# A Winograd convolution: the fourth input pair by SyncE's queue in fp32, the fifth's casting load issued later

## The chip, the cores and the metric

The kernel runs on one core of a Trainium2 chip. The metric is the device time of one execution in microseconds (us), the median of three runs. A profile of one execution, taken by the hardware profiler, goes with it.

## The reference

A 3x3 convolution with padding 1, stride 1, no bias: 16 images of 64 channels, 64 x 64 pixels, to 128 channels. Inputs and output are fp32.

```python
batch, c_in, h, w, c_out = 16, 64, 64, 64, 128
x_pad = np.pad(x, ((0, 0), (0, 0), (1, 1), (1, 1)), mode='constant')
...
output[b, co] += weight[co, ci, kh, kw] * x_pad[b, ci, kh:kh+h, kw:kw+w]
```

The input is 16.8 MB, the output 33.6 MB.

## The kernel before

**Pairs.** Two images of 64 channels fill the 128 partitions, so there are 8 pairs, counted from index 0 in the code ("the fourth pair" is index 3). One pair is 2.10 MB of fp32, 16 KB in each partition. Each image of a pair is multiplied with 64 rows of TensorE.

**The transform.** The convolution is taken two output rows at a time. The input rows stay in fp16 in `xs[p]`; `ss[p]` holds the sums of the row pairs (rows 2j and 2j+1). The weights are combined once into five groups in `Wt` (G0, G21, G1, G01, G2). For each pair there are four blocks (`blk`) of 8 row pairs. A block computes three products for both images: U (G1 on `ss`), A (G21 and G0 on `xs`) and Bt (G01 and G2 on `xs`), each in a PSUM tile `acc` for each image; one line, L174, holds all these matmuls. ScalarE copies U to `ut` (L188); VectorE adds A + U into the even output rows (L196) and Bt + U into the odd ones (L199) of the output tile `ot`.

**The input's two ways.** The first three pairs come in fp32 by SyncE's queue into tiles `x0`, `x1`, `x2` of the pool `opool` (L43 to L47), and are cast to `xs` on the chip, in pieces of 16 rows (L104): pair 0 by ScalarE and GpSimd, pairs 1 and 2 by ScalarE alone, at blocks that the table `later` names. The other five pairs come by loads that GpSimd issues and that cast to fp16 on the way (`load`, L60): indices 3 and 4 after GpSimd's own casts of pair 0, indices 5 to 7 behind the sums of the third pair. `load(q, H)` is one transfer of a whole pair, `load(q, H // 2)` two of half a pair.

**Sums.** Pair 0's sums are made on VectorE. GpSimd makes those of pair p + 1 at the start of the loop's turn p, in two halves (L73), from the fp32 tile where there is one in `raws`, else from `xs`.

**Output.** `opool` has seven buffers of 16 KB in a partition, shared by the fp32 input tiles and the output tiles `ots` (two for each pair, one for each image). They are handed out in turn, so that an output tile waits for whatever used its buffer seven tiles earlier. Image 0 of a pair is stored by SyncE's queue, image 1 by ScalarE's, the latter one block late (`held`). Most stores are a whole image (2.10 MB); image 0 of the first pair and both images of the last are stored in halves (`cuts_of`).

**Order.** The framework places the waits between engines; `keep(...)` holds an instruction in program order on its engine. `spool` has three buffers for `ss`, `xpool` eight for `xs`, so no `xs` is reused.

Of the kernel before, what the change touches and what calls it, by code (L numbers as in the profile page):

```python
# [8 lines left out]
F32 = mybir.dt.float32  # L9
F16 = mybir.dt.float16  # L10
# [3 lines left out]
def kernel(  # L14
# [6 lines left out]
    nc = tc.nc  # L21
    B, CI, H, W = x.shape
    CO = weight.shape[0]
    assert H == 64 and W == 64 and CI == 64 and CO == 128 and B % 2 == 0
    NP = B // 2
# [3 lines left out]
    x_rows = x.rearrange("b c h w -> (b c) h w")  # L29
# [5 lines left out]
    xpool = ctx.enter_context(tc.tile_pool(name="xpool", bufs=8))  # L35
    opool = ctx.enter_context(tc.tile_pool(name="opool", bufs=7))
# [7 lines left out]
    x1 = opool.tile([128, H, W], F32, tag="ot", name="x1")  # L44
    nc.sync.dma_start(x1, x_rows[128:256, :, :])
    x2 = opool.tile([128, H, W], F32, tag="ot", name="x2")
    nc.sync.dma_start(x2, x_rows[256:384, :, :])  # L47
    raws = {1: x1, 2: x2}
    ident = const.tile([128, 128], F16)
    make_identity(nc, ident)  # L50
    w16 = const.tile([CO, CI * 9], F16)
    keep(nc.gpsimd.tensor_copy(w16, w_raw))  # L52

    xs = {p: xpool.tile([128, H, W], F16, tag="xs", name="xs") for p in range(3)}

    def load(p, rows):
        xs[p] = xpool.tile([128, H, W], F16, tag="xs", name="xs")
        for lo in range(0, H, rows):
            keep(
                nc.gpsimd.dma_start(  # L60
                    xs[p][:, lo : lo + rows, :],
                    x_rows[128 * p : 128 * p + 128, lo : lo + rows, :],
                )
            )
# [3 lines left out]
    def sums(eng, p, src, lo, n):  # L68
        if p not in ss:
            ss[p] = spool.tile([128, H // 2, W], F16, tag="ss", name="ss")  # L70
        v = src.rearrange("p (j i) c -> p j i c", i=2)
        keep(
            eng.tensor_add(  # L73
                ss[p][:, lo : lo + n, :], v[:, lo : lo + n, 0, :], v[:, lo : lo + n, 1, :]
            )
        )
# [26 lines left out]
    def cast(copy, p, src, lo, hi):  # L103
        keep(copy(xs[p][:, lo:hi, :], src[:, lo:hi, :]))  # L104
# [5 lines left out]
    keep(nc.scalar.copy(wrow(G2), wps[2]))  # L110
    cast(nc.gpsimd.tensor_copy, 0, x0, 34, 50)
    cast(nc.gpsimd.tensor_copy, 0, x0, 50, 64)
    for p in (3, 4):
        load(p, H)
    later = {
        (0, 0): [(0, x0, 18, 34)],
        (0, 2): [(1, x1, 0, 16), (1, x1, 16, 32)],
        (0, 3): [(1, x1, 32, 48), (1, x1, 48, 64)],
    }
    later.update({(1, n): [(2, x2, 16 * n, 16 * n + 16)] for n in range(4)})  # L120

    held = []

# [4 lines left out]
    def store(eng, p, b2, ot, lo, hi):  # L128
        return eng.dma_start(
            out_rows[2 * p + b2, :, lo:hi, :],  # L130
            ot.rearrange("p j i c -> p (j i) c")[:, lo:hi, :],
        )

    for p in range(NP):
        if p + 1 < NP:
            for lo in (0, 16):
                sums(nc.gpsimd, p + 1, raws.get(p + 1, xs[p + 1]), lo, 16)
                if (p, lo) == (1, 16):
                    for q in range(5, NP):
                        load(q, H if q == 5 else H // 2)  # L140
        ots = [
            opool.tile([128, H // 2, 2, W], F32, tag="ot", name="ot") for _ in range(2)
        ]
        for blk in range(4):
            j0 = blk * RB

            def group(wi_rows):

                tiles = [
                    psum.tile([128, RB, W], F32, tag="acc", name="acc") for _ in range(2)  # L150
                ]
                n = 3 * len(wi_rows)
                i = 0
                for wi, off in wi_rows:
                    for kw in (1, 0, 2):
                        c_lo, c_hi = max(0, 1 - kw), min(W, W + 1 - kw)
                        for b2 in range(2):
                            p0 = 64 * b2
                            lo, hi = j0, j0 + RB
                            if off is None:  # L160
                                rhs = ss[p][p0 : p0 + 64, lo:hi, c_lo + kw - 1 : c_hi + kw - 1]
                            else:
                                while 2 * lo + off < 0:
                                    lo += 1
                                while 2 * (hi - 1) + off > H - 1:
                                    hi -= 1
                                first = 2 * lo + off
                                last = 2 * (hi - 1) + off
                                rhs = xs[p][
                                    p0 : p0 + 64,  # L170
                                    first : last + 1 : 2,
                                    c_lo + kw - 1 : c_hi + kw - 1,
                                ]
                            nc.tensor.matmul(  # L174
                                tiles[b2][:, lo - j0 : hi - j0, c_lo:c_hi],
                                Wt[p0 : p0 + 64, wi, kw, :],
                                rhs,
                                start=i == 0,
                                stop=i == n - 1,
                            )  # L180
                        i += 1
                return tiles

            U = group([(G1, None)])
            us = []
            for b2 in range(2):
                ut = upool.tile([128, RB, W], F32, tag="ut", name="ut")
                keep(nc.scalar.copy(ut, U[b2]))  # L188
                us.append(ut)
            while held and (p, blk) != (1, 0):  # L190
                keep(store(nc.scalar, *held.pop(0)))
            for piece in later.get((p, blk), ()):
                cast(nc.scalar.copy, *piece)
            A = group([(G21, 1), (G0, -1)])
            for b2 in range(2):
                nc.vector.tensor_add(ots[b2][:, j0 : j0 + RB, 0, :], A[b2], us[b2])  # L196
            Bt = group([(G01, 0), (G2, 2)])
            for b2 in range(2):
                nc.vector.tensor_add(ots[b2][:, j0 : j0 + RB, 1, :], Bt[b2], us[b2])  # L199
            if blk in cuts_of[p][0]:  # L200
                store(nc.sync, p, 0, ots[0], *cuts_of[p][0][blk])
            if blk in cuts_of[p][1]:
                held.append((p, 1, ots[1], *cuts_of[p][1][blk]))
# [32 lines left out]
```

## Time and profile before

| what | value |
|---|---|
| median of 3 runs | 125.97 us (125.95 to 126.64) |
| the profiled execution's own time | 126.62 us |
| its span, first to last instruction | 124.8 us |
| TensorE busy | 108.0 us (86% of the span) |
| VectorE, ScalarE, GpSimd busy | 84.5, 46.5, 38.6 us |
| HBM read, written | 17.07 MB, 33.55 MB |
| transfers, share of 16 engines: SyncE's, ScalarE's, GpSimd's queue | 45.0%, 31.7%, 20.8% |
| mean granted TensorE clock | 0.961 |

The queues appear in the profile as q1 (SyncE), q10 (ScalarE) and q0 (GpSimd). Their MB are bytes written: a casting load of a pair counts 1.05 MB although it reads 2.10 MB. The share of 16 engines is the time that a queue's packets took, as a part of what the core's 16 transfer engines had. The profiled execution lies 0.65 us above the median; 1.8 us of its time lie outside its span. Windows are given in us from the start of the span.

### The profile page before, as it was taken

What the parts mean: (1) busy time and instruction counts of PE and PEld (TensorE: products, weight loads), DVE (VectorE), ACT (ScalarE), POOL (GpSimd) and SP (SyncE); (2) the same over time, 40 slices, a digit from 0 to 9 for tenths busy, and PEclk for the clock granted to TensorE, in tenths of its full rate; (3) what the DMA queues carried; (4) which work ended last, traced back from release to release, by engine and by line L of the source; (5) the groups of instructions that cost most, each with busy time, mean ns of one, the idle gap of its engine ahead of it and who ended that gap; (6) DMA issues with size and microseconds to landing.
All of it is one profiled execution on the core that took longest, in us unless ns stands there. A gap on an engine that the chain in (4) does not pass through costs nothing.

```text
span 124.8 us, 2430 instructions
## 1 busy us (share of the span) xinstructions
PE 108.0 (86%) x984; PEld 49.8 (40%) x984; DVE 84.5 (68%) x135; ACT 46.5 (37%) x78; POOL 38.6 (31%) x30
## 2 busy tenths in 40 slices
PE   0699999999999999999999999999999999990000
PEld 0544444444444444444444444444444444430000
DVE  1019987877777887888777778777877787774000
ACT  4118559966653333333333333333333333330000
POOL 2219780799975001910240032004200510000000
PEclk9999999999999999999999999999999999999555
DMA  5899999999999999999999999999999999999991
GB/s 163 367 430 451 430 302 247 278 276 312 365 344 333 341 370 385 382 392 375 370 381 386 382 400 369 354 406 400 374 369 404 425 420 430 420 420 430 428 404 68
DMA packets 4330, 45.52 MB, mean 365 GB/s; under 512 B 480, under 2 KB 480, under 8 KB 1120
## 3 DMA queue, kind: packets, MB, share of 16 engines
q1 hardware_dynamic: 2016, 23.36, 45.0%
q10 hardware_dynamic: 1296, 16.78, 31.7%
q0 software_dynamic: 1008, 5.24, 20.8%
q8 instruction: 7, 0.11, 0.3%
q14 instruction: 3, 0.02, 0.0%
HBM read 17.07 MB, written 33.55 MB: 406 GB/s over the span
## 4 chain that ended last, share of the span: by engine, by line
PE 86%; DMA 2%; DVE 1%; issue 1%; POOL 1%; DVEq 0%
PE acc L174 81%; PE warm L97 3%; DMA w_raw<-in_weight_dram 2%; PE wp L91 1%; DVE ot L196 1%; POOL w L52 1%; DVEq L231 0%; DVE ot L199 0%; DVEq L196 0%
## 5 line engine op out<-in xcount | busy, mean ns | idle before, releaser
L174 PE MATMUL acc<-xs,Wt 64*128 64x504 f16 (+3 forms) x768 | 87.0, 374 | 0.0
L174 PEld LDWEIGHTS <-Wt 64*128 64x128 f16 x960 | 46.9, 95 | 56.2 <-issue 0.9
L188 ACT COPY ut<-acc 128x512 f32<-128x512 f32 x64 | 34.4, 589 | 56.9 <-issue 39.0
L196 DVE TENSOR_TENSOR ot<-acc,ut 128x512 f32<-128x512 f32 x64 | 41.2, 685 | 20.8 <-PE acc L174 18.4
L199 DVE TENSOR_TENSOR ot<-acc,ut 128x512 f32<-128x512 f32 x64 | 41.1, 683 | 0.0
L73 POOL TENSOR_TENSOR ss<-xs 128x1024 f16<-128x1024 f16 x10 | 21.1, 2130 | 49.3 <-DMA xs<-in_x_dram 49.3
L174 PE MATMUL acc<-ss,Wt 64*128 64x504 f16 (+1 forms) x192 | 26.0, 377 | 0.0
L104 ACT CAST xs<-x 128x1024 f16<-128x1024 f32 (+1 forms) x10 | 10.5, 1070 | 3.3 <-DMA x<-in_x_dram 3.3
L73 POOL TENSOR_TENSOR ss<-x 128x1024 f16<-128x1024 f32 x4 | 9.4, 2358 | 5.0 <-DMA x<-in_x_dram 5.0
L73 DVE TENSOR_TENSOR ss<-x 128x512 f16<-128x512 f32 x4 | 3.3, 868 | 7.5 <-DMA x<-in_x_dram 7.5
L91 PE MATMUL wp<-ident,w 128*64 128x128 f16 x18 | 1.3, 328 | 4.3 <-POOL w L52 4.3
L104 POOL CAST xs<-x 128x1024 f16<-128x1024 f32 (+1 forms) x2 | 3.0, 1518 | 4.5 <-DMA x<-in_x_dram 4.5
L97 PE MATMUL warm<-blank 128*128 128x400 f32 x6 | 4.2, 864 | 0.0
L60 POOL DMA_DIRECT2D xs<-in_x_dram x7 | 3.9, 574 | 0.0
L91 PEld LDWEIGHTS <-w 128*64 128x64 f16 x18 | 1.1, 210 | 4.3 <-POOL w L52 4.3
L97 PEld LDWEIGHTS warm<-blank 128*128 128x128 f32 x6 | 1.8, 326 | 1.4 <-issue 1.3
L98 ACT CAST Wt<-wp 128x384 f16<-128x384 f32 x1 | 0.5, 478 | 3.0 <-PE wp L91 3.0
L98 ACT ACT_TABLE_LOAD x1 | 1.3, 1283 | 0.7 <-PEq L220 0.7
L52 POOL CAST w<-w_raw 128x576 f16<-128x576 f32 x1 | 0.7, 663 | 2.3 <-DMA w_raw<-in_weight_dram 2.3
L94 DVE MEMSET blank<- 128x400 f32 x1 | 0.4, 392 | 0.9 <-PEq L220 0.9
L109 ACT CAST Wt<-wp 128x384 f16<-128x384 f32 x1 | 0.5, 478 | 0.5 <-DVE Wt L101 0.5
L100 DVE TENSOR_TENSOR Wt<-wp,Wt 128x384 f16<-128x384 f32 x1 | 0.6, 551 | 0.0
(8 smaller groups left out, 1.9 us busy)
## 6 DMA issues: line engine op xcount, KB each, us to landing
out_dram<-ot ACTq DMA_DIRECT2D x7, 2048.0 KB, 19.0
out_dram<-ot SPq DMA_DIRECT2D x6, 2048.0 KB, 18.3
x<-in_x_dram SPq DMA_DIRECT2D x3, 2048.0 KB, 12.0
out_dram<-ot SPq DMA_DIRECT2D x4, 1024.0 KB, 12.6
xs<-in_x_dram POOLq DMA_DIRECT2D x3, 1024.0 KB, 22.0
xs<-in_x_dram POOLq DMA_DIRECT2D x4, 512.0 KB, 51.2
out_dram<-ot ACTq DMA_DIRECT2D x2, 1024.0 KB, 11.1
w_raw<-in_weight_dram SPq DMA_DIRECT2D x1, 288.0 KB, 2.8
```

What stands on the lines that cost most here:

```text
L52: keep(nc.gpsimd.tensor_copy(w16, w_raw))
L60: nc.gpsimd.dma_start(xs[p][:, lo : lo + rows, :], x_rows[128 * p : 128 * p + 128, lo : lo + rows, :],)
L73: eng.tensor_add(ss[p][:, lo : lo + n, :], v[:, lo : lo + n, 0, :], v[:, lo : lo + n, 1, :])
L91: nc.tensor.matmul(wp[q : q + 64, k * CO : k * CO + CO], w16[:, t::9], ident)
L97: nc.tensor.matmul(warm[:, 0:400], blank[:, 0:128], blank)
L98: keep(nc.scalar.copy(wrow(G1), wps[1]))
L100: keep(nc.vector.tensor_sub(wrow(G21), wps[2], wrow(G1)))
L104: keep(copy(xs[p][:, lo:hi, :], src[:, lo:hi, :]))
L174: nc.tensor.matmul(tiles[b2][:, lo - j0 : hi - j0, c_lo:c_hi], Wt[p0 : p0 + 64, wi, kw, :], rhs, start=i == 0, stop=i == n - 1,)
L188: keep(nc.scalar.copy(ut, U[b2]))
L196: nc.vector.tensor_add(ots[b2][:, j0 : j0 + RB, 0, :], A[b2], us[b2])
L199: nc.vector.tensor_add(ots[b2][:, j0 : j0 + RB, 1, :], Bt[b2], us[b2])
```

## The change

The fourth pair (index 3) is loaded in fp32 into a further `opool` tile `x3` by SyncE's queue, right behind `x2`; its cast to `xs[3]` is done by ScalarE in four pieces in the four blocks of pair index 2, and GpSimd makes its sums from `x3`. The fifth pair's casting load (index 4) is issued behind the second pair's sums (loop turn 0) instead of ahead of the loop. The loads of indices 5 to 7 stay behind the third pair's sums and keep their sizes. The output tiles move by one place in the turn of the seven buffers.

```diff
     x2 = opool.tile([128, H, W], F32, tag="ot", name="x2")
     nc.sync.dma_start(x2, x_rows[256:384, :, :])
-    raws = {1: x1, 2: x2}
+    x3 = opool.tile([128, H, W], F32, tag="ot", name="x3")
+    nc.sync.dma_start(x3, x_rows[384:512, :, :])
+    raws = {1: x1, 2: x2, 3: x3}
...
-    xs = {p: xpool.tile([128, H, W], F16, tag="xs", name="xs") for p in range(3)}
+    xs = {p: xpool.tile([128, H, W], F16, tag="xs", name="xs") for p in range(4)}
...
-    for p in (3, 4):
-        load(p, H)
...
-    later.update({(1, n): [(2, x2, 16 * n, 16 * n + 16)] for n in range(4)})
+    for p in (2, 3):
+        later.update({(p - 1, n): [(p, raws[p], 16 * n, 16 * n + 16)] for n in range(4)})
...
                 sums(nc.gpsimd, p + 1, raws.get(p + 1, xs[p + 1]), lo, 16)
-                if (p, lo) == (1, 16):
-                    for q in range(5, NP):
-                        load(q, H if q == 5 else H // 2)
+                if lo == 16 and p < 2:
+                    for q in ((4,), range(5, NP))[p]:
+                        load(q, H if q < 6 else H // 2)
```

## The prediction

> **What bounds the kernel now.** I read the chain of waits first, because it names the engine that seems to set the end:
>
> ```profile
> PE 86%; DMA 2%; DVE 1%; issue 1%; POOL 1%; DVEq 0%
> ```
>
> Taken alone this says TensorE. But TensorE's last instruction lies near 113 us and the span is 124.8 us, so I read the slices and the queue table of the page next:
>
> ```profile
> PE   0699999999999999999999999999999999990000
> DMA  5899999999999999999999999999999999999991
> ...
> q1 hardware_dynamic: 2016, 23.36, 45.0%
> q10 hardware_dynamic: 1296, 16.78, 31.7%
> q0 software_dynamic: 1008, 5.24, 20.8%
> ```
>
> TensorE is busy without a gap and then stops; the transfer engines go on for about 10 us more. The three queues' packets take 45.0 + 31.7 + 20.8 = 97.5% of 16 engines' span. q1 is SyncE's queue (fp32 loads, half of the stores), q10 ScalarE's (the other stores), q0 GpSimd's (casting loads). The table of windows shows how full the transfer engines are stage by stage (the last two columns are their share and the GB/s written):
>
> ```profile
> 5.00:15.00 10.00, 10.00 (x68) 4.67 (x66) 6.22 (x10) 5.46 (x9) 5.44 (x5) 1.00 1.02 436
> 15.00:30.00 15.00, 15.00 (x144) 6.89 (x142) 12.37 (x21) 10.18 (x15) 10.77 (x10) 1.00 1.01 282
> 30.00:50.00 20.00, 20.00 (x192) 9.21 (x190) 15.37 (x25) 9.12 (x16) 8.98 (x5) 1.00 1.02 356
> 50.00:100.00 50.00, 50.00 (x472) 22.92 (x470) 39.26 (x63) 16.17 (x31) 11.76 (x6) 1.00 1.02 386
> 100.00:113.00 13.00, 12.30 (x116) 5.47 (x112) 10.24 (x18) 4.29 (x8) 0.34 (x1) 1.00 1.00 425
> 113.00:121.00 8.00, 0.00 (x0) 0.00 (x0) 0.67 (x2) 0.00 (x0) 0.00 (x0) 0.64 1.01 426
> ```
>
> From 5 to 121 us the share is never under 1.00. The end is the end of the transfers. How much TensorE could slip before it matters comes from the transfers after 113 us:
>
> ```profile
> DMA packets 544, 3.86 MB, mean 322 GB/s; under 512 B 74, under 2 KB 74, under 8 KB 74
> ...
> out_dram<-ot SPq DMA_DIRECT2D x1, 1024.0 KB, 10.5
> out_dram<-ot ACTq DMA_DIRECT2D x1, 1024.0 KB, 10.2
> ```
>
> The last two stores, 1.05 MB each, are issued at 113.1 and 113.7 us. 3.86 - 2.10 = 1.76 MB were still queued ahead of them, 1.76 MB / 426 GB/s = **4.1 us of backlog**. A compute delay below that costs nothing at the end; a change in transfer work counts in full.
>
> **The change, part by part.**
>
> *The fourth pair's transfer.* Both forms read 2.10 MB of fp32 from HBM; the casting form writes 1.05 MB, the SyncE form 2.10 MB. From the windows of the transfers: in 15 to 30 us q0 took 62.6% of 15 us for 1.85 MB, 5.08 us per MB written, so the fourth pair's casting load cost 1.049 x 5.08 = 5.33 us of all 16 engines. (Over 30 to 100 us it is 23.6% of 70 us for 3.39 MB, 4.87 us per MB, 5.11 us a pair.) An fp32 load on q1 in 5 to 15 us: 101.9% of 10 us for 4.36 MB, 2.34 us per MB, 2.10 x 2.34 = 4.90 us. In 15 to 30 us q1, shared with casts, paid 38.3% of 15 us for 2.36 MB, 2.43 us per MB, 5.10 us a pair. The saving lies between 5.11 - 5.10 = 0.0 and 5.33 - 4.90 = 0.43 us. Most of the new load runs while SyncE's queue is alone, as in the 5 to 15 us row, and what it replaces ran in the 15 to 30 us row, so I take 0.4 us. Upper bound with everything around it: source bytes moved in 15 to 30 us are 4.23 + 1.85 = 6.08 MB, 405 GB/s against 436 before it; if the whole stretch ran at 436, it would save 15 x (1 - 405/436) = 1.07 us.
>
> *The fifth pair's issue* moves from 12.3 us (L60 after the two POOL casts at L104) to behind the second pair's sums. Rows:
>
> ```profile
> 13.73 4.68 POOL L73 TENSOR_TENSOR ss<-x 128x1024 f16<-128x1024 f32 x2 [0.75 <-DMA x<-in_x_dram]
> 22.63 4.68 POOL L73 TENSOR_TENSOR ss<-x 128x1024 f16<-128x1024 f32 x2 [4.23 <-DMA x<-in_x_dram]
> 27.26 2.69 POOL L60 DMA_DIRECT2D xs<-in_x_dram  x5
> ```
>
> The two POOL issues at 11.74 us took 1.24 us; without them the second pair's sums (data landed 13.7) still wait for their data, so nothing is gained there. The fifth's load is issued at about 18.4 us and takes 0.56 us of POOL. The third pair's fp32 no longer shares the engines: the first two landed at 8.8 and 13.7 us, so it lands near 18.7 instead of 22.6. Its sums run to about 23.9, and the loads of pairs 6 to 8 go out about 3.5 us earlier. No cost: the sums for the fourth pair need ss[0]'s slot and x3, the fifth's the cast load; both land long before TensorE needs them (50 and 63 us).
>
> *Casts.* Four ScalarE pieces of 1.06 us (L104) join blocks (2,0) to (2,3), 4.2 us. The same pieces sit in blocks (1,0) to (1,3) now, and TensorE runs on there without a gap; ScalarE then idles 1.2 us a block. The sums of pair 4 read fp32: 2 x (2.36 - 2.12) = 0.5 us more of POOL, which waits 49.3 us for loads in all. If that cover were gone, the casts would still have the 4.1 us of backlog. SyncE's extra issue is 0.43 us at 2.5 us, ahead of nothing but the store at 17.15 us.
>
> *The stores behind x3.* This is the real risk. In 50 to 75 us the queues take turns packet by packet: nearly equal counts, half the time for the half-size loads:
>
> ```profile
> q1 hardware_dynamic: 289, 4.21, 40.2%
> q10 hardware_dynamic: 291, 4.24, 39.9%
> q0 software_dynamic: 299, 1.09, 21.6%
> ```
>
> So a queue progresses by rounds. Eight packets per engine make a pair's transfer: 4.90 / 8 = 0.61 us a whole fp32 packet, half that for half-tile stores, 5.2 / 8 = 0.65 us a casting one. Now the first image's half stores (issued 17.15 and 23.9 us) land 13.0 and 18.9 us later, at 30.2 and 42.8. With x3 ahead of them: x3 runs alone from 18.7 until casting packets appear, 3.3 us after the issue as now (issued 11.74, first packets after 15), at 21.7; the remaining 1.9 us then goes at half rate, to 25.4. First half store: two rounds of 0.31 + 0.65 to 27.4, where ScalarE's store joins, then six of 0.31 + 0.61 + 0.65 = 1.57, to 36.8; second: eight more of 1.57, or of 1.24 once half-size casts follow (0.31 + 0.61 + 0.33), so it ends at 48.5 to 49.4 and lands, some 0.8 us later, at **49.3 to 50.2 us**. The same count for the kernel before gives 42.4 against the 42.8 shown. Its `ot` slot is taken again by the second image of pair index 3, whose first addition starts at 50.22 + 0.61 = 50.8 us:
>
> ```profile
> 50.22 1.29 DVE L196 TENSOR_TENSOR ot<-acc,ut 128x512 f32<-128x512 f32 x2 [0.58 <-ACT ut L188]
> ```
>
> The margin shrinks from 8.0 us to 0.6 to 1.5 us. Next comes SyncE's store of pair index 1, eight rounds of 0.61 + 0.61 + 0.33: near 62 us, needed at 50.8 + 12.8 = 63.6. I cost it at nothing; a miss of 2 us would be hidden by the backlog.
>
> *Sum:* -0.4 us of transfer work, +0 elsewhere. The profiled execution took 126.62 us (124.8 of span, 1.8 around it), giving 126.2; it is 0.65 above the median of 125.97. Against the median: **125.6 us**. I take 1% (1.26 us) as what a measurement of this kernel can tell from no change.
>
> **The rivals.**
>
> *A. The mixed stretch clears up: faster.* The 405 GB/s in 15 to 30 us may be what whole-pair casting loads, one behind the other, cost everything beside them. Then the full 1.07 us comes back, and with it the slower part of 30 to 50 us, where the sixth pair's whole-pair load runs (356 GB/s written and 1.38 MB of casts, 425 GB/s of source bytes; 20 x (1 - 425/436) = 0.5 us): 125.97 - 1.6 = 124.4. For it: no other stretch is as slow, and in it both q0 and q1 cost more per MB than elsewhere. Against: the fifth and sixth pairs' whole-pair casts still run from 21.7 us on.
>
> *B. A late slot: slower.* Place: vector addition L196 of pair index 3, second image, waiting for the second half store. If x3's eight packets share three ways (0.61 + 0.65 + 0.61 = 1.87 us each), the store is late by 15 us instead of 7: 57.8 us. DVE then waits 7.0 us, PSUM tiles aren't freed, TensorE stops, and every later store shifts. It counts beyond 4.1 us: 125.97 + 2.9 - 0.4 = 128.5; a store landing at 56.5 gives 127.2. Against: ScalarE's first store is issued only at 26.7 us, after x3 is nearly in.
>
> *C. Written bytes count: slower.* If the engines' price follows the bytes written, x3 costs 1.05 MB more at 436 GB/s, 2.4 us: 128.4. Against: 15 to 30 us writes only 282 GB/s at a share of 1.01, so casts fill the engines by what they read. The Trainium skill, "DMA: Bandwidth & Descriptors", section "Where 436 GB/s comes from", says the SBUF ports bind at 435 GB/s; by that rule this rival would hold wherever the ports are full. The trace agrees with the ceiling (436 in 5 to 15 us) but shows the engines full far below it under casts.
>
> *D. Nothing at all:* the packets cost the same either way, 126.0. This lies inside the forecast's own range.
>
> **How the numbers follow.** Forecast with D, 125.6, own range 125.0 to 126.6: 0.56. A: 0.19. B: 0.15, spread from 126.8 to 128.5. C: 0.10. Faster by over 1% needs A: 0.19. Slower by over 1% (over 127.2) needs C or most of B: 0.23; within 1%: 0.58. The range reaches to A's end and into half of B: 124.3 to 127.7.
>
> **What would show it.** Right: the transfer share stays at 1.00 from 5 to 121 us; q0 falls by 1.05 MB and about 4.3% of the span, q1 rises by 2.10 MB and 4%; the third pair's sums start near 18.7 instead of 22.6; the second half store takes about 26 us to land; TensorE still ends near 113. Wrong: L196 or TensorE with more than 4 us of idle time released by out_dram (B); q1's cost per MB above 2.5 us while x3 moves (C); 15 to 30 us at 425 GB/s of source bytes or more (A).

## The result and the profile after

The changed kernel takes **136.4 us** (median of 6 runs, 136.18 to 137.99) against 126.17 us for the kernel before in the same runs: 1.083 times as long, 95% interval 1.077 to 1.089. The prediction was 125.6 us. Its profiled execution took 136.34 us, 134.6 us of it span.

The chain of waits of the changed kernel, shares by engine and by line (PE is TensorE, DVE VectorE, ACT ScalarE, POOL GpSimd; L175, L197 and L200 are L174, L196 and L199 of the kernel before):

```profile
PE 67%; DMA 20%; DVE 3%; issue 1%; DVEq 1%; POOL 1%
PE acc L175 63%; DMA out_dram<-ot 18%; PE warm L99 3%; DMA w_raw<-in_weight_dram 2%; DVE ot L197 2%; PE wp L93 1%; DVE ot L200 1%; POOL w L54 1%; DVEq L232 0%; DVEq L197 0%
```

An output store now has 18% of the chain, and it was not in it before. In order of time (start, length, what; "..." where pieces are left out) the chain shows which store:

```profile
10.20 11.82 PE acc L175 x108
...
23.99 24.34 DMA out_dram<-ot
...
48.86 0.70 DVE ot L197
...
49.60 72.99 PE acc L175 x638
```

The store issued at 23.99 us is the second half of pair index 0's first image, on SyncE's queue. It lands 24.34 us later, at 48.33 us, and releases an addition into an output tile, which releases TensorE. VectorE's timeline names the place (start, length, and in brackets the idle time before it and what ended it):

```profile
38.06 0.69 DVE L197 TENSOR_TENSOR ot<-acc,ut 128x512 f32<-128x512 f32 x1 [0.70 <-POOL ss L75]
48.86 0.69 DVE L197 TENSOR_TENSOR ot<-acc,ut 128x512 f32<-128x512 f32 x1 [10.10 <-DMA out_dram<-ot]
```

These are the first two additions of block (2,0): the first image's at 38.06 us, the second image's after a wait of 10.1 us. In the kernel before the two stand together:

```profile
37.46 1.29 DVE L196 TENSOR_TENSOR ot<-acc,ut 128x512 f32<-128x512 f32 x2 [0.63 <-PE acc L174]
```

The table of waits of the changed kernel adds what followed on TensorE (total, times, longest):

```profile
DVE ot L197 <- DMA out_dram<-ot: 10.1, 1, 10.1
PE acc L175 <- DVE ot L197: 8.3, 1, 8.3
```

The stages, as the table of windows shows them for the changed kernel (length, busy time of PE, of its weight loads, of DVE, ACT and POOL, then granted TensorE clock, share of the transfer engines, GB/s written):

```profile
30.00:50.00 20.00, 11.71 (x110) 5.05 (x106) 7.75 (x13) 8.15 (x12) 5.70 (x3) 0.86 1.02 355
50.00:100.00 50.00, 50.00 (x450) 25.05 (x448) 38.27 (x62) 17.99 (x32) 12.61 (x6) 0.95 0.88 333
100.00:113.00 13.00, 13.00 (x126) 6.62 (x122) 10.05 (x17) 4.29 (x8) 0.00 (x0) 1.00 0.77 324
```

Up to 50 us the transfer engines are as full as before while TensorE stands still. Then the stores that were not computed in time are missing, and the casting loads take their place: from 50 to 75 us GpSimd's queue writes 1.78 MB, where it wrote 1.09 MB before (packets, MB, share).

```profile
q0 software_dynamic: 499, 1.78, 35.5%
```

From 75 to 100 us it has nothing left to write, where it wrote 0.91 MB before, and between the late stores the engines run dry: 0.12 x 50 + 0.23 x 13 = 9.0 us idle from 50 to 113 us, of the 9.8 us by which the span grew (134.6 - 124.8).

TensorE's granted clock also fell, some 3 us into the stop that began at 41.3 us. In windows of 1 us it was 1.00 from 43 to 44 us, 0.73 from 44 to 45, 0.50 from 45 to 54, 0.65 from 54 to 55, and 1.00 from 55 us on. So the matmuls that started again at 49.60 us ran at half the clock for about 5 us:

```profile
45.00:50.00 5.00, 0.40 (x3) 0.14 (x4) 1.14 (x2) 0.00 (x0) 0.00 (x0) 0.50 1.03 392
50.00:55.00 5.00, 5.00 (x28) 2.12 (x26) 3.23 (x6) 1.72 (x3) 0.00 (x0) 0.53 1.01 385
```

The last addition of the whole kernel ends 11.5 us later than before, at 125.2 instead of 113.7 us:

```profile
112.39 1.28 DVE L199 TENSOR_TENSOR ot<-acc,ut 128x512 f32<-128x512 f32 x2
123.89 1.28 DVE L200 TENSOR_TENSOR ot<-acc,ut 128x512 f32<-128x512 f32 x2
```

TensorE's stop is 8.3 us of this. Half of the 5 us at half the clock, 2.5 us, is an estimate for the slow restart, and the loop's first matmul started 0.5 us later than in the chain of the kernel before (10.20 against 9.74 us); together that is 11.3 us.

So the open question was: why does a tile of pair index 2 wait for a store of pair index 0, when the prediction had that store's buffer used again only by pair index 3, 12.8 us later?

### The profile page after: what moved, and what is told of

It reads as the page before. It is cut to its first block, busy times and chain, and to the rows that moved or that the text cites. A ratio compares the mean times of both kernels' runs of the same rounds, so it can differ in the third digit from the quotient of the medians.

```text
span 134.6 us, 2434 instructions
## 1 busy us (share of the span) xinstructions
PE 111.1 (83%) x984; PEld 54.0 (40%) x984; DVE 84.6 (63%) x135; ACT 50.4 (37%) x82; POOL 38.5 (29%) x29
## 4 chain that ended last, share of the span: by engine, by line
PE 67%; DMA 20%; DVE 3%; issue 1%; DVEq 1%; POOL 1%
PE acc L175 63%; DMA out_dram<-ot 18%; PE warm L99 3%; DMA w_raw<-in_weight_dram 2%; DVE ot L197 2%; PE wp L93 1%; DVE ot L200 1%; POOL w L54 1%; DVEq L232 0%; DVEq L197 0%
## 5 line engine op out<-in xcount | busy, mean ns | idle before, releaser
L175 PE MATMUL acc<-xs,Wt 64*128 64x504 f16 (+3 forms) x768 | 93.8, 379 | 8.3 <-DVE ot L197 8.3
L175 PEld LDWEIGHTS <-Wt 64*128 64x128 f16 x960 | 51.0, 96 | 63.6 <-issue 12.0
L197 DVE TENSOR_TENSOR ot<-acc,ut 128x512 f32<-128x512 f32 x64 | 41.3, 685 | 32.1 <-PE acc L175 18.9
L200 DVE TENSOR_TENSOR ot<-acc,ut 128x512 f32<-128x512 f32 x64 | 41.1, 683 | 0.0
L175 PE MATMUL acc<-ss,Wt 64*128 64x504 f16 (+1 forms) x192 | 31.3, 386 | 0.0
L75 POOL TENSOR_TENSOR ss<-xs 128x1024 f16<-128x1024 f16 x8 | 16.8, 2122 | 39.1 <-PE acc L175 19.6
L106 ACT CAST xs<-x 128x1024 f16<-128x1024 f32 (+1 forms) x14 | 14.7, 1066 | 3.1 <-DMA x<-in_x_dram 3.1
L75 POOL TENSOR_TENSOR ss<-x 128x1024 f16<-128x1024 f32 x6 | 14.1, 2365 | 2.4 <-DMA x<-in_x_dram 2.4
L62 POOL DMA_DIRECT2D xs<-in_x_dram x6 | 3.4, 579 | 0.0
```

The costliest lines, as they stand in the source:

```text
L62: nc.gpsimd.dma_start(xs[p][:, lo : lo + rows, :], x_rows[128 * p : 128 * p + 128, lo : lo + rows, :],)
L75: eng.tensor_add(ss[p][:, lo : lo + n, :], v[:, lo : lo + n, 0, :], v[:, lo : lo + n, 1, :])
L175: nc.tensor.matmul(tiles[b2][:, lo - j0 : hi - j0, c_lo:c_hi], Wt[p0 : p0 + 64, wi, kw, :], rhs, start=i == 0, stop=i == n - 1,)
```

## The experiments

**The program's own waits** gave the theory. In the instruction list of the changed kernel, the late addition waits on the completion of two transfers, the sixth and seventh issued on the SyncE and ScalarE queues (counting w as number 1 and x3 as number 5): the two half stores of pair index 0's first image. Listing all first writes to output tiles with the transfers that they wait for gives who took whose buffer (s00 is the store of pair index 0's image 0, and so on):

```
            before             changed
pair 2      x0, x1             x1, s00
pair 3      s00, s01           s01, x2
pair 4      x2, s10            s10, s11
pair 5      s11, s20           x3, s20
```

The description ahead of the prediction says that the seven buffers are handed out in turn. That is wrong: the list reads as an order in which buffers are given back (x0, x1, s00, s01, x2, s10, s11 and so on), and in it x2, allocated first, stands behind both of pair index 0's output tiles. The tiles' addresses in the two built programs give the same table. That the framework keeps such an order is read off these two lists and not shown in another way. Before, two of the seven buffers were still unused for pair index 1, pair index 2 took x0 and x1, and the first reuse of a stored tile came at pair index 3. With x3 in the pool one buffer is unused, pair index 1 takes x0 already, and pair index 2 gets x1 and s00.

Theory 1 is then: the buffer costs the time. Rival 2: the transfers' new order does, whatever buffer is used. Rival 3: the later issue of the fifth pair's load does.

**Buffers by hand, strictly in turn, in the changed kernel.** One pool of one buffer for each of the seven, and a table:

```diff
-    opool = ctx.enter_context(tc.tile_pool(name="opool", bufs=7))
+    bufs = [ctx.enter_context(tc.tile_pool(name=f"o{k}", bufs=1)) for k in range(7)]
+    BUF = [((4 + 2 * p) % 7, (5 + 2 * p) % 7) for p in range(8)]
...
-            opool.tile([128, H // 2, 2, W], F32, tag="ot", name="ot") for _ in range(2)
+            bufs[k].tile([128, H // 2, 2, W], F32, tag="ot", name="ot") for k in BUF[p]
```

x0 to x3 take buffers 0 to 3.

> The changed kernel, with each of the seven 16 KB buffers named by hand and given out strictly in turn (tile k takes buffer k modulo 7), as the prediction assumed. Theory 1 (buffer): the whole loss comes from pair index 2's second output tile being given the buffer of the first image of pair index 0, whose second half store lands only at 48.3 us; in turn it takes x2's buffer, the 10.1 us wait is gone, and the time is what the prediction said, 125.2 to 126.5 us; the half store still lands near 48 to 50, within 2 us of its next use at 51. Rival 2 (queue order): fp32 ahead of the stores on SyncE's queue and the later casting loads leave the transfer engines idle later on whatever buffer is used: 131 us or more, with the transfer share still under 0.9 from 70 to 115 us.

Measured: 126.42 us, 1.0029 times the kernel before (1.0018 to 1.0039). No addition waits for a store any more; the windows of this kernel:

```profile
50.00:100.00 50.00, 50.00 (x474) 22.47 (x470) 38.91 (x63) 16.84 (x32) 9.30 (x5) 1.00 1.02 392
100.00:113.00 13.00, 12.96 (x122) 5.66 (x118) 10.24 (x17) 4.30 (x8) 0.00 (x0) 1.00 1.00 419
```

The engines are full again to the end: the shares are 1.02 and 1.00 where the changed kernel had 0.88 and 0.77. The second half store is still late, 23.8 us from issue to landing against 24.3 in the changed kernel and 18.9 before. The transfers' new order alone loses 0.36 us and the buffer 10 us. Rival 2 falls.

**Only the fourth pair's way changed**: x3 by SyncE's queue with its casts and sums, the fifth's load back ahead of the loop.

```diff
+    load(4, H)
     later = {
...
-                if lo == 16 and p < 2:
-                    for q in ((4,), range(5, NP))[p]:
-                        load(q, H if q < 6 else H // 2)
+                if (p, lo) == (1, 16):
+                    for q in range(5, NP):
+                        load(q, H if q == 5 else H // 2)
```

> The fourth pair in fp32 by SyncE's queue as in the changed kernel, the fifth's casting load issued ahead of the loop as in the kernel before. Theory 1: the order in which buffers come free is the same as in the changed kernel, so the same tile waits for the same half store, 8 to 13 us: 134 to 139 us. Rival 3 (issue): the later issue of the fifth's load is to blame: about 126 us.

Measured: 1.0847 times the kernel before (1.0826 to 1.0869); the profiled execution took 136.61 us. Same tile, same store, a slightly longer wait (this kernel's L198 and L176 are the changed kernel's L197 and L175):

```profile
DVE ot L198 <- DMA out_dram<-ot: 11.3, 1, 11.3
PE acc L176 <- DVE ot L198: 9.5, 1, 9.5
```

**Only the fifth pair's issue moved**, in the kernel before.

```diff
-    for p in (3, 4):
-        load(p, H)
+    load(3, H)
...
-                if (p, lo) == (1, 16):
-                    for q in range(5, NP):
-                        load(q, H if q == 5 else H // 2)
+                if lo == 16 and p < 2:
+                    for q in ((4,), range(5, NP))[p]:
+                        load(q, H if q < 6 else H // 2)
```

> The kernel before with only the issue of the fifth pair's casting load moved behind the second pair's sums; the fourth's stays a casting load at its old place. Theory 1: no buffer changes hands, no wait appears: 125.6 to 126.8 us. Rival 3: 132 us or more.

Measured: 126.04 us, ratio 1.0001 (0.9987 to 1.0016). Rival 3 falls: the whole loss belongs to the fourth pair's new way, its tile and its transfer.

**Only the early buffer**, in the kernel before: buffers by hand as above, all as the pool gave them, but for pair index 2's second tile and pair index 3's first, which change places.

```diff
+    BUF = [(3, 4), (5, 6), (0, 3), (1, 4), (2, 5), (6, 0), (3, 1), (4, 2)]
```

> The kernel before, its transfers and casts untouched, with buffers named by hand: all as before, but pair index 2's second output tile takes the buffer of pair index 0's first image (and pair index 3's first tile x1's buffer instead). Theory 1: VectorE waits at about 38.1 us for the half store that lands at 42.8 us, 4.7 us. What this costs at the end tells two readings of the slack apart: if 4.1 us of backlog hide it, as the prediction said, 126.5 to 127.2 us; if only 1.1 us are hidden (tail of 11.1 us after the last addition before, 10.0 us in the changed kernel), 129 to 130.5 us. Rival 2: 126 us, the buffer doesn't matter.

> The kernel with the early buffer once more, for the profile of an execution near its median of 126.7 us. If the wait for the half store is 4 to 5 us there too while the end moves by 0.7 us, the slack is near 4 us; if the wait is short (under 2 us), the slack is small and the store landed earlier in those executions.

Measured: 126.71 us in the first run, ratio 1.006 (1.003 to 1.009). Two executions were profiled. In one, of 126.44 us, the wait is 3.1 us:

```profile
41.38 0.69 DVE L197 TENSOR_TENSOR ot<-acc,ut 128x512 f32<-128x512 f32 x1 [3.10 <-DMA out_dram<-ot]
```

In the other, of 129.74 us and so 2.4% above the median, the wait is 4.6 us and the last addition 4.8 us later than before; it is left out of the comparison below.

So the early buffer does make this addition wait without any new transfer, but for 3.1 us only, and it costs 0.66 us at the median. The large loss takes both: the buffer one pair early, and x3 ahead of the store on the same queue. The store lands at 41.3 us in the execution of 126.44 us, at 42.8 in the profile of before, and at 48.3 in the changed kernel.

The slack, the delay of the compute that the end hides, is not settled by this. The 126.71 us lie in the range that was expected for 4.1 us hidden (126.5 to 127.2), but that range was built on a wait of 4.7 us; and 3.1 us lies between the two cases that the second expectation set apart. The next two kernels tell more.

**A delay of the compute alone**, in the kernel before: extra additions on VectorE in block (2,0), into a scratch tile `scr`, eight in one kernel and sixteen in the other.

```diff
+            if (p, blk) == (2, 0):
+                for _ in range(8):
+                    keep(nc.vector.tensor_add(scr, us[0]..., us[1]...))
             for b2 in range(2):
                 nc.vector.tensor_add(ots[b2][:, j0 : j0 + RB, 0, :], A[b2], us[b2])
```

> The kernel before with eight extra additions of 128x512 fp32 (about 0.68 us each, 5.4 us together) into a scratch tile on VectorE in the first block of pair index 2; nothing else is changed, no transfer and no buffer. They put the compute 4 to 5 us behind, as the early buffer did. If the end hides a delay up to the 4.1 us of the prediction: 126.2 to 127.0 us. If only 1.1 us are hidden: 129 to 130.5 us.

> The same with sixteen extra additions, 10.9 us together, so the compute is put some 10 us behind, as in the changed kernel, but without its reordered transfers. If the delay of the compute is the whole cause, the end moves by the delay less the slack: with 4.1 us hidden 131 to 133 us, with 1.1 us hidden 134 to 136 us, and the transfer share falls under 0.9 after 55 us as in the changed kernel. If the reordered transfers have a part in the loss, clearly less than the changed kernel's 136.4 us even after allowing for the length of the delay.

Measured: 129.07 us, ratio 1.023 (1.017 to 1.028), and 139.26 us, ratio 1.100 (1.093 to 1.108). Sixteen additions delayed the compute by 15.2 us, not 10, so that expectation's numbers don't apply as they stand; its form does. The granted clock was 0.50 to 0.60 there from 44 to 48 us and from 58 to 64 us, which lengthens the delay as in the changed kernel. The end of the last addition, read from each kernel's VectorE timeline, beside the span of the same execution (for the early buffer the one of 126.44 us):

```
                       last addition ends   later by   span    from there to the end
before                 113.7                 -         124.8   11.1
early buffer           115.2                 1.5       124.7    9.5
eight additions        118.6                 4.9       128.0    9.4
changed kernel         125.2                11.5       134.6    9.4
sixteen additions      128.8                15.2       138.1    9.3
```

One rule fits all five within 0.1 us: the end is at 124.7 us or 9.4 us behind the last addition, whichever is later. The slack in the profiled execution of before is 11.1 - 9.4 = 1.7 us (the 1.1 us of the expectations set 10.0 us for the changed kernel, which is 9.4 when counted from the same point); that execution is 0.6 us above the median of 126.05, by which the slack is nearer 1.1 us, and eight additions end just inside the range that was expected for 1.1. The medians alone (129.07 against 126.11 us in the same runs, for a delay of 4.9 us) would give 1.9 us. So the slack is known as 1 to 2 us, and 4.1 us is ruled out.

The changed kernel has the same 9.4 us behind its last addition as the kernels that only delay the compute. Once its compute is late, then, the new transfers add nothing to the end that this table shows: 11.5 - 1.7 = 9.8 us is the whole growth of the span. With sixteen additions the transfer engines run dry as they do in the changed kernel (share 0.51 from 85 to 90 us, 0.44 from 100 to 105).

## Why the prediction was wrong, point by point

*What bounds the kernel: right.* The transfers bind the kernel before. The kernels with the buffers in turn, with only the issue moved and with the early buffer had their last addition 0.7, 0.1 and 1.5 us later in the executions read here, and none of their medians is more than 0.7 us from that of the kernel before.

*The step that failed: "Its `ot` slot is taken again by the second image of pair index 3".* The landing, though 1.0 to 1.9 us too late, was near: 49.3 to 50.2 us forecast, 48.3 measured. It was not luck, since the working holds at the first half store too: 36.8 + 0.8 = 37.6 us by it, 36.6 measured. But the buffer's next user was pair index 2, at 38.7 us instead of 50.8. The wait of 10.1 us that followed was put at nothing. The rule came from the description ahead of the prediction, and the profile of before could not refute it: with buffers in turn, pair index 3's first tile would have had x2's buffer there, in fact it had that of pair index 0's first image, and no addition waited for a store either way. An idle time of zero doesn't show which buffer a tile uses. The waits written into the instructions do.

*Rival B was the mechanism, with the wrong place and the wrong store time.* It had VectorE wait at pair index 3 for a store at 57.8 us; the wait was one pair earlier, for a store at 48.3 us. Its chance was 0.15, and its worst price, 128.5 us, was far too low in both of its terms: a wait of 7.0 us, where the compute came 11.5 us late, and 4.1 us of it hidden, where 1 to 2 us are.

*The slack: 4.1 us forecast, 1 to 2 us measured.* The bytes left at 113 us were read as backlog. They belonged to the stores of pair index 6, issued at 100 us and later, and to the first halves of pair index 7: had the compute been later, they would have been issued later too. From the issue of pair index 6's stores on, 8.4 MB remain, 8.4 / 0.426 = 19.7 us of transfers, while pair index 7 takes 12.8 us to compute; so by this estimate at least 6.9 us of transfers lie behind the last addition however empty the queues were. The 9.4 us of the table are 2.5 us more; issue, landing and a last stretch in which the engines are no longer full belong to them, but no run takes them apart. Only what was still queued ahead of that burst was slack.

*The transfer term: -0.4 us forecast, no saving measured.* In the kernel with the buffers in turn the three queues' shares are 49.2 + 31.7 + 16.8 = 97.7% of 124.6 us, 121.7 us; before, 97.5% of 124.8 us, 121.7 us. The lower of the two bounds, 0.0, was right. From 15 to 30 us q1 paid 2.42 us per MB there (64.9% for 4.03 MB) and the casting load 5.26 (36.5% for 1.04 MB). By these prices the fourth's load won 5.33 - 2.10 x 2.42 = 0.25 us and the fifth's lost 1.05 x (5.26 - 5.08) = 0.19 us, an estimate that leaves nearly nothing. With the buffers in turn rival D, nothing at all, comes nearest. That this kernel is 0.36 us slower than before is measured, but what part of it does that is open.

*Rivals A and C: no.* Source bytes from 15 to 30 us moved at 401 GB/s in the changed kernel (5.00 + 1.02 MB) and 409 in the one with buffers in turn, not 425 or more; q1 stayed at 2.43 us per MB (64.3% for 3.97 MB), under the 2.5 that C needed.

*The smaller steps held.* The fifth's load went out at 18.35 us; the third pair's sums followed at 19.07 us; the last loads at 23.70, 3.6 us earlier:

```profile
18.35 0.70 POOL L62 DMA_DIRECT2D xs<-in_x_dram  x1
19.07 4.70 POOL L75 TENSOR_TENSOR ss<-x 128x1024 f16<-128x1024 f32 x2
23.70 2.69 POOL L62 DMA_DIRECT2D xs<-in_x_dram  x5
```

ScalarE's four casts cost nothing: with them, and with the buffers in turn, TensorE is busy for all of the 20 us from 30 to 50.

## What to carry to other kernels

One more tile in a shared pool moves every later tile to another buffer: before adding it, list for each tile whose buffer it takes and when that one's last reader (often a store) is done, from the waits of the built program and not from the order of allocation. A full queue at the end is not slack if its stores come from the compute that would be late; the slack is what lies ahead of the last burst, and a delay put into the compute measures it. In this kernel a stop of the compute that outlasted the slack turned the bound from the transfers to the compute: the loads ran ahead meanwhile and left nothing to fill the gaps between the stores.

## What the runs showed of the hardware

A casting load from GpSimd cost the transfer engines about what it reads. In the changed kernel it took 4.8 us per MB written from 30 to 50 us (33.6% for 1.40 MB) and 5.4 from 15 to 30 us (36.6% for 1.02 MB), which is 2.4 to 2.7 us per MB read, against 2.34 to 2.43 us per MB on SyncE's queue. So casting on the way saved no transfer time here.

In the changed kernel's stop of 8.3 us TensorE's granted clock stayed at 1.00 for some 3 us and then fell to 0.50; it was back at 1.00 some 5 us after the matmuls had started again.
